# A tenth set of seven block products in a fused mixer layer, with decayed queries and keys kept in place

## The chip, the cores and the metric

One Trainium2 chip, one of its cores. The metric is the device time of one execution, in microseconds, from the first to the last instruction of the program and what lies around it. The kernel has the tensor engine (PE), the vector engine (DVE), the scalar engine (ACT), GpSimd (POOL) and the sync engine (SP) to itself; all data are float32 in HBM.

## The reference

One layer, 256 tokens, model width 2048. A normalised input is multiplied by one wide matrix, its columns are split into the operands of two mixers, and the mixers' results are projected, gated, summed and projected again:

```python
h = rmsnorm(x, pre_norm_g[l])
proj = h @ w_in[l]                      # 2048 x 18448
(a_q, a_k, a_v, a_g, a_lr, b_q, b_k, b_v, b_g, m_a, m_b) = jnp.split(proj, offsets, axis=-1)
gk = jax.nn.log_sigmoid((a_lr @ gla_gk_w2[l] + gla_gk_b[l])) / GATE_LOGIT_NORMALIZER
o_a = gla_chunked(...)                  # linear attention with a decay per key channel
o_a = rmsnorm(o_a, gla_norm_g[l]).reshape(B, S, GLA_VAL_DIM) * jax.nn.silu(a_g)
y_a = o_a @ w_branch_a[l]
o_b = diff_attention(...)               # difference of two softmax attentions
y_b = o_b @ w_branch_b[l]
merged = jax.nn.sigmoid(m_a) * y_a + jax.nn.sigmoid(m_b) * y_b
out = merged @ w_out[l]
x = x + rmsnorm(out, post_norm_g[l])
```

The 2048 columns of m_a, the gate of the linear-attention branch, are the ones that this change moves.

## The kernel before, in words

**Precision by splitting.** Each float32 weight block of 1024 columns per partition is split into a high and a low part: `hi` is a copy by ACT (line 356), `lo` is the rest, by a DVE subtraction (line 357). A product is three matmuls: hi by the input's high part, hi by its low part, lo by its high part. `hi` and `lo` have three buffers each, so a block can be split at most about two blocks ahead of its use. The unit of work is a *half step*: one split, and the matmuls that use it.

**Three kinds of half step.** In a token-major half tile (`half_tile`) 12 matmuls of 512 columns are made; in a channel-major one (`half_channel`) 8 of 512 and 8 of 256; both take as long. In a *set* a half step has 6 matmuls of 512, since a set multiplies blocks by seven products instead of eight (Winograd's form of Strassen's scheme): 1024 weight columns, seven products of 1024 x 512 blocks in the order `PRODUCTS = (1, 3, 5, 6, 2, 7, 4)`, each in four half steps (two tiles `t`, two halves `h`). Products 3, 5, 6 and 7 use sums of input blocks, kept as `s4`, `r1`, `s2`, `r3`. A set has 28 half steps, so 168 matmuls; the plain way takes 192 for the same 1024 columns.

**What a set costs beside matmuls.** Sums of weight blocks: some are made by an accumulating DMA on POOL's queue (line 249), eight per set by DVE, 1024 elements each (line 257, `a<-a,b` and `a<-a,c`). The DVE adds of products 7's tiles stand right behind each `lo` of product 7 in DVE's order. After product 6 and after product 7 DVE adds 512 columns of the product's bank to a kept one (`gr`, lines 880 and 889), both at a raised priority of the scheduler.

**The set phase.** `phase_steps` writes the order by hand: nine sets, and between their half steps 64 half steps of other work (*partners*): the last value columns, the linear attention's keys and queries, three of eight pairs of the other attention's heads. `PARTNERED` lists eight places in a set, each behind a (product, tile), that take a partner; `ALONE` takes places away. Before, set 0 has nine partners (two of them at its front), sets 1 to 7 have seven, set 8 has six. In this phase the order on PE is pinned.

**The phase after.** Plain work: two gates of 512 columns (`m02`, `m03`, 8 half tiles each), between them the five remaining head pairs (40 half tiles), then the projection `y0` (28 of its half tiles). Between these, *background tasks* get a turn: `pump(LANES)` gives the next step to each of the first three tasks of a list. A turn comes after every second half tile; a task that asked for it (`eager`) gets one in between. First in the list are `gla_scores(0)` and `(1)` (18 and 19 steps), then `gla_out`, then two lanes of the other attention. `gla_out` fetches values that were spilled (`vback`, on POOL's queue, in program order with the spills `dh` and `dl` of the heads), weighs them by the scores (line 526) and must be over when `y0` begins.

**Linear attention, before.** Scores come in seven levels of block size m = 1 to 64. Two running sums of log decays, `pre` and `suf`, are grown from level to level by DVE adds (lines 966, 967); at each level ACT takes their exponentials and DVE multiplies them into a copy of the queries (`xq`) and keys (`xk`). The products of `xq` and `xk` go to PE (line 982).

Of the kernel before, what the change touches and what calls it, by code (L numbers as in the profile page):

```python
# [10 lines left out]
AF = mybir.ActivationFunctionType  # L11
# [3 lines left out]
P = 128  # L15
# [11 lines left out]
ROWS = {"two": 2, "tok": 4, "chan": KT}  # L27
WARM = 10
PRODUCTS = (1, 3, 5, 6, 2, 7, 4)
SETS = 9  # L30
MERGE = (0, 1, 6)
GLA_GATES = (7, 8)
LEAD = 6
PAIRS = [(g, pair) for g in range(4) for pair in range(2)]
EARLY = 3
PARTNERED = ((1, 1), (3, 1), (5, 1), (6, 0), (6, 1), (2, 1), (7, 0), (7, 1))
SPILL_AT = (6, 0, 0)
ALONE = tuple((s, 6, 1) for s in range(9)) + ((8, 3, 1),)
# [15 lines left out]
def chunk_plan():  # L54

    plan = [("v0", "two", "w_in", [(6144, RANK), (2048, 2 * VG[0] - RANK)])]
    at = 2 * VG[0] - RANK
    for g, n in enumerate(VG[2:]):
        plan.append((f"v{g + 2}", "tok", "w_in", [(2048 + at, n)]))
        at += n  # L60
    for hf in range(2):
        for name, base in (("k", 1024), ("q", 0)):
            for c in range(4):
                plan.append((f"{name}{hf}{c}", "chan", "w_in", [(base + 512 * hf + P * c, P)]))
    o = 6144 + RANK
    for s in range(2):
        plan.append((f"set{s}", "set", "w_in", [(o + 10240 + 1024 * s, 1024)]))
    for s in range(2, 6):
        plan.append((f"set{s}", "set", "w_in", [(o + base + 512 * (s - 2), 512) for base in (4096, 6144)]))
    plan.append(("set6", "set", "w_in", [(o + 8192, 1024)]))  # L70
    for i, s in enumerate(GLA_GATES):
        plan.append((f"set{s}", "set", "w_in", [(4096 + 1024 * i, 1024)]))
    for g in range(4):
        for c in range(4):
            for n, name in enumerate(("dq", "dk")):
                plan.append((f"{name}{g}{c}", "chan", "w_in", [(o + 2048 * n + 512 * g + P * c, P)]))
        if g > 1:
            plan.append((f"m0{g}", "tok", "w_in", [(o + 8192 + 512 * g, 512)]))
        for br in range(2):
            kind = "late" if br and g < 2 else "tok"  # L80
            plan.append((f"y{br}{g}", kind, ("w_branch_a", "w_branch_b")[br], [(512 * g, 512)]))
        plan.append((f"o{g}", "late", "w_out", [(512 * g, 512)]))
    plan.append(("ys0", "half", "w_branch_b", [(c, 512) for c in BRANCH_COLS]))
    for s, cols in enumerate(LATE_COLS):
        plan.append((f"os{s}", "half", "w_out", [(c, 512) for c in cols]))
    return plan
# [56 lines left out]
def hybrid_kernel(ctx: ExitStack, tc, xt, xn, preg, postg, w, w2, gkb, glag, lamv, diffg, ident_d, causal_d, lmask_d, out):  # L143
# [57 lines left out]
    def halves_of(*keys):  # L201
        return [(key, r, h) for key in keys for r in range(len(at[key])) for h in range(2)]
# [2 lines left out]
        return halves_of(*(f"{name}{g}{c}" for g, pair in pairs for name in ("dq", "dk") for c in (2 * pair, 2 * pair + 1)))  # L205

    seq = halves_of("v0", "v2", "v3") + phase_steps()
    seq += halves_of("m02") + heads_order(PAIRS[EARLY:]) + halves_of("m03", *(f"y0{g}" for g in range(4)))[:-4]
    seq += branch_steps() + late_steps() + halves_of("o2", "o3")
    ready = {}  # L210
    emitted = [0]
# [288 lines left out]
        return xs[kt // 2][:, kt % 2].rearrange("p i t -> p (i t)")  # L500

    tasks = []
    ts, heads, m0 = {}, {}, []
    DONE = object()
    done = set()
    latest = [None]
# [49 lines left out]
    def half_tile(banks, n, q, ops, hi, lo, begin=0):  # L556
        for w, parts in ((hi, (0, 1)), (lo, (0,))):
            for j in range(2):
                kt = 2 * q + j
                a = ops(kt)  # L560
                for b in range(2):
                    for part in parts:
                        first, last = kt == begin and w is hi and part == 0, kt == KT - 1 and w is lo
                        i = mm(banks[b][:, :n], a[part][:, P * b : P * b + P], w[:, n * j : n * j + n], start=first, stop=last)
        latest[0] = i.ins

    def token_major(key, n, ops, step=1, upto=KT // 2):
        banks = [ps("mm"), ps("mm")]
        for q in range(upto):
            half_tile(banks, n, q, ops, *take(key))  # L570
            if q % 2 or not ts:
                pump(step)
            else:
                pump_eager()
        return banks

    def half_channel(o, h, hi, lo):
        turns = [(w, j) for w in (hi, lo) for j in range(8)]
        if h:
            turns.append(turns.pop(7))  # L580
        for w, j in turns:
            kt, c = 8 * h + j, slice(P * j, P * j + P)
            if w is hi:
                i = mm(o, hi[:, c], x_pair(kt), start=kt == 0, stop=kt == KT - 1)
            else:
                i = mm(o[:, :S], lo[:, c], x_ops(kt)[0], start=False, stop=False)
        latest[0] = i.ins

    def channel_major(key):
        o = ps("mm")  # L590
        for h in range(2):
            half_channel(o, h, *take(key))
            if h == 0:
                pump_eager()
        return o[:, :S], o[:, S:]

    def gate(bank, b, dst):
# [161 lines left out]
    def merge_gate(banks):
        t = u2([P, 2, 512], "mgate")  # L760
        for b in range(2):
            act.activation(t[:, b, :], banks[b], AF.Tanh, scale=half_rstd[:, b : b + 1])
        m0.append(spill(t, "mgate"))

    def head_part(t, o, o2, scaled):
        act.activation(t, o2, AF.Copy)
        dve.tensor_tensor(out=t, in0=o, in1=t, op=ALU.add)
# [155 lines left out]
    def gla_scores(hf):  # L923
# [1 line left out]
        if hf:  # L925
            yield
        pre = gp[hf]
        suf = u2([P, 2, 4, P], "suf")
        aall = u2([P, 3, 2, P], "att")
        a = aall[:, :2]  # L930
        ah, al = u2([P, 3, 2, P], "ath", F32R), u2([P, 3, 2, P], "atl", F32R)
# [12 lines left out]
        pool.memset(suf, 0.0)
        yield
        for n, m in enumerate(LEVELS):
            segs = 256 // m
# [4 lines left out]
            if m > 1:  # L952
                xk = t2([P, 512], "xk")
                xkv = view(xk, 0, (m, 2), (2 * m, segs), (1, m))
            act.activation(xqv, view(pre, m, *late), AF.Exp, scale=1.0 / 16.0)
            dve.tensor_tensor(out=xqv, in0=xqv, in1=view(q, m, *late), op=ALU.mult)
            if m == 1:
                dve.tensor_tensor(out=xqv, in0=xqv, in1=view(k, 0, *early), op=ALU.mult)
                add_pairs(es[:, 512:], xq, 64)
                act.activation(eh, es, AF.Copy)  # L960
                dve.tensor_tensor(out=el, in0=es, in1=f32(eh), op=ALU.subtract)
                pool.memset(a, 0.0)
            else:
                act.activation(xkv, view(suf, 0, *early), AF.Exp, scale=1.0 / 16.0)
                dve.tensor_tensor(out=xkv, in0=xkv, in1=view(k, 0, *early), op=ALU.mult)
            dve.tensor_tensor(out=view(suf, 0, *early), in0=view(suf, 0, *early), in1=view(pre, 2 * m - 1, (513 - 2 * m, 2), (2 * m, segs), (0, m)), op=ALU.add)
# [19 lines left out]
        xq = t2([P, 512], "xq")  # L986
        xk = t2([P, 512], "xk")
        flat = "p c t -> p (c t)"
        act.activation(xq, pre[:, 1].rearrange(flat), AF.Exp, scale=1.0 / 16.0)
        dve.tensor_tensor(out=xq, in0=xq, in1=q[:, 1].rearrange(flat), op=ALU.mult)  # L990
        act.activation(xk, suf[:, 0].rearrange(flat), AF.Exp, scale=1.0 / 16.0)
        dve.tensor_tensor(out=xk, in0=xk, in1=k[:, 0].rearrange(flat), op=ALU.mult)
        yield
# [665 lines left out]
```

## Time and profile before

| | |
|---|---|
| median of 3 runs | 1082.58 us (1082.48 to 1083.47) |
| the profiled execution's own time | 1083.89 us |
| its span | 1082.1 us |
| PE busy | 1073.0 us, 99% |
| DVE busy | 948.0 us, 88% |
| ACT busy | 741.8 us, 69% |
| DMA | 293.44 MB, mean 271 GB/s |

Busy time is the union of the instructions' spans, and matmuls overlap, so a busy PE may have short waits inside. A wait is better seen in the starts of the matmuls: where PE waits for nothing they follow at a fixed distance. The page numbers lines of the kernel before; the changed kernel's lines are some four to eleven higher.

### The profile page before, as it was taken

What the parts mean: (1) busy time and instruction counts of PE and PEld (TensorE: products, weight loads), DVE (VectorE), ACT (ScalarE), POOL (GpSimd) and SP (SyncE); (2) the same over time, 40 slices, a digit from 0 to 9 for tenths busy, and PEclk for the clock granted to TensorE, in tenths of its full rate; (3) what the DMA queues carried; (4) which work ended last, traced back from release to release, by engine and by line L of the source; (5) the groups of instructions that cost most, each with busy time, mean ns of one, the idle gap of its engine ahead of it and who ended that gap; (6) DMA issues with size and microseconds to landing.
All of it is one profiled execution on the core that took longest, in us unless ns stands there. A gap on an engine that the chain in (4) does not pass through costs nothing.

```text
span 1082.1 us, 15375 instructions
## 1 busy us (share of the span) xinstructions
PE 1073.0 (99%) x5404; PEld 919.1 (85%) x5404; DVE 948.0 (88%) x1282; ACT 741.8 (69%) x1068; POOL 168.1 (16%) x249
## 2 busy tenths in 40 slices
PE   9999999999999999999999999999999999999997
PEld 8998888888888888888888888888888888888886
DVE  7788999899999989998999999977778878889885
ACT  7987767677677767677777665556777776565662
POOL 0202121121212121212112200031011011100000
PEclk9999999999999999999999999999999999999999
DMA  9899889899989989898988766699898898988752
GB/s 346 285 324 300 261 250 345 206 311 271 276 291 212 332 202 390 177 381 188 350 190 274 295 226 205 211 325 302 285 278 276 279 288 277 319 302 259 276 191 91
DMA packets 67213, 293.44 MB, mean 271 GB/s; under 512 B 8704, under 2 KB 11776, under 8 KB 49984
## 3 DMA queue, kind: packets, MB, share of 16 engines
q1 hardware_dynamic: 38656, 174.29, 45.5%
q0 software_dynamic: 27904, 117.45, 40.1%
q8 instruction: 42, 0.69, 0.2%
q10 hardware_dynamic: 576, 0.73, 0.2%
q14 instruction: 35, 0.29, 0.1%
HBM read 265.17 MB, written 27.26 MB: 270 GB/s over the span
## 4 chain that ended last, share of the span: by engine, by line
PE 85%; issue 8%; DVE 3%; DMA 2%; POOL 1%; ACT 0%; POOLq 0%; SPq 0%; DVEq 0%; ACTq 0%
PE mm L553 57%; PE bg L553 20%; PE mm L541 2%; PE bg L541 2%; DVE lo L357 2%; DMA vback<-vl 1%; DMA raw<-in_w_dram 1%; PE bg L1149 0%; PE bg L1123 0%; PE bg L526 0%; PE bg L1124 0%; POOL dl L177 0%; DVE keep L357 0%; PE bg L1161 0%; PE bg L1162 0%
## 5 line engine op out<-in xcount | busy, mean ns | idle before, releaser
L356 ACT ACTIVATE hi<-raw 128x1024 fp32r<-128x1024 f32 (+3 forms) x229 | 234.8, 1028 | 152.9 <-PE mm L553 74.2
L357 DVE TENSOR_TENSOR lo<-raw,hi 128x1024 fp32r<-128x1024 f32 (+3 forms) x231 | 271.0, 1179 | 35.1 <-ACT hi L356 32.0
L356 ACT ACTIVATE hi<-a 128x1024 fp32r<-128x1024 f32 x144 | 152.5, 1061 | 54.8 <-PE mm L553 32.1
L357 DVE TENSOR_TENSOR lo<-a,hi 128x1024 fp32r<-128x1024 f32 x144 | 171.9, 1218 | 7.0 <-ACT hi L356 5.4
L553 PE MATMUL mm<-hi,xs 128*128 128x512 f32 (+1 forms) x688 | 174.7, 383 | 0.0
L553 PEld LDWEIGHTS mm<-hi,xs 128*128 128x128 f32 x688 | 128.5, 188 | 21.5
L553 PE MATMUL bg<-xs,hi 128*128 128x512 f32 x448 | 115.4, 390 | 0.0
L357 DVE TENSOR_TENSOR lo<-b,hi 128x1024 fp32r<-128x1024 f32 x72 | 87.9, 1221 | 18.0 <-ACT hi L356 16.0
L553 PE MATMUL mm<-lo,xs 128*128 128x512 f32 (+1 forms) x344 | 98.6, 383 | 0.1
L553 PEld LDWEIGHTS bg<-xs,hi 128*128 128x128 f32 x448 | 84.2, 188 | 16.4
L356 ACT ACTIVATE hi<-b 128x1024 fp32r<-128x1024 f32 x72 | 76.1, 1059 | 25.8 <-PE mm L553 13.7
L553 PE MATMUL mm<-xs,hi 128*128 128x512 f32 x320 | 84.9, 397 | 0.0
L553 PEld LDWEIGHTS mm<-lo,xs 128*128 128x128 f32 x344 | 64.2, 188 | 12.1 <-DVE lo L357 1.2
L553 PEld LDWEIGHTS mm<-xs,hi 128*128 128x128 f32 x320 | 57.7, 189 | 9.7
L553 PEld LDWEIGHTS bg<-xs,lo 128*128 128x128 f32 x448 | 61.0, 190 | 5.0 <-DVE lo L357 0.7
L553 PE MATMUL bg<-xs,lo 128*128 128x256 f32 x448 | 62.6, 283 | 0.3 <-DVE lo L357 0.3
L249 POOL DMA_DIRECT2D b<-in_w_dram x36 | 31.0, 861 | 152.7 <-DVE a L257 76.2
L356 ACT ACTIVATE hi<-c 128x1024 fp32r<-128x1024 f32 x36 | 38.2, 1062 | 21.5 <-PE bg L553 12.7
L553 PE MATMUL mm<-hi,oah 128*128 128x512 f32 x128 | 50.8, 397 | 0.0
L553 PE MATMUL mm<-hi,oal 128*128 128x512 f32 x128 | 50.0, 391 | 0.0
L357 DVE TENSOR_TENSOR lo<-c,hi 128x1024 fp32r<-128x1024 f32 x36 | 43.1, 1219 | 5.0 <-ACT hi L356 5.0
L553 PEld LDWEIGHTS mm<-xs,lo 128*128 128x128 f32 x320 | 43.6, 190 | 3.2
(410 smaller groups left out, 2218.5 us busy)
## 6 DMA issues: line engine op xcount, KB each, us to landing
raw<-in_w_dram SPq DMA_DIRECT2D x98, 1024.0 KB, 7.3
c<-in_w_dram SPq DMA_DIRECT2D x36, 512.0 KB, 8.9
a<-in_w_dram POOLq DMA_DIRECT2D x36, 512.0 KB, 9.7
b<-in_w_dram POOLq DMA_DIRECT2D x36, 512.0 KB, 7.3
a<-in_w_dram POOLq DMA_DIRECT2D x16, 1024.0 KB, 13.2
b<-in_w_dram POOLq DMA_DIRECT2D x16, 1024.0 KB, 8.7
raw<-in_w_dram SPq DMA_DIRECT2D x14, 832.0 KB, 7.4
gr<-gr POOLq DMA_DIRECT2D x9, 512.0 KB, 8.6
```

Source lines behind the costliest of these rows:

```text
L249: tc.keep_in_program_order(pool.dma_start(chain[s, name, i][:, c], block(s, 1, i)[:, c], accum_op=ALU.add))
L356: act.activation(hi_t[:, a:b], r[:, a:b], AF.Copy)
L357: dve.tensor_tensor(out=lo_t[:, a:b], in0=r[:, a:b], in1=f32(hi_t[:, a:b]), op=ALU.subtract)
L541: i = pe.matmul(banks[g][b][:, :n], a[part][:, P * b : P * b + P], w[:, n * g : n * g + n], start=first, stop=last)
L553: i = pe.matmul(*args, **kw)
```

## The change

Three things change.

1. The last 1024 columns of m_a (two plain gates of 512 columns) become a tenth set (set 7; the linear attention's gates move to sets 8 and 9). `merge_gate` goes, and the new set's two result tiles are spilled and fetched like those of set 6. The 64 partners stay, and now have ten sets: `ALONE` takes the place behind (2, 1) away from sets 2 to 9 and the place behind (6, 1) from all, so sets 2 to 9 have six partners each.
2. The linear attention keeps queries and keys decayed in place: at each level DVE multiplies `q` and `k` by a decay that ACT took from a sum of log decays over the level's segments (`total`, halved in width from level to level); `xq` and `xk` become copies by ACT.
3. Background turns come from `tick`: each half step adds 2/3 after its hi matmuls and 1/3 after its lo matmuls, and every 1.5 of this one turn is given to the first three tasks. The extra turns of eager tasks go.

```diff
-SETS = 9
-MERGE = (0, 1, 6)
-GLA_GATES = (7, 8)
+SETS = 10
+MERGE = (0, 1, 6, 7)
+GLA_GATES = (8, 9)
...
-ALONE = tuple((s, 6, 1) for s in range(9)) + ((8, 3, 1),)
+ALONE = tuple((s, 6, 1) for s in range(10)) + tuple((s, 2, 1) for s in range(2, 10))
+PACE = 1.5
...
-    seq += halves_of("m02") + heads_order(PAIRS[EARLY:]) + halves_of("m03", *(f"y0{g}" for g in range(4)))[:-4]
+    seq += heads_order(PAIRS[EARLY:]) + halves_of(*(f"y0{g}" for g in range(4)))[:-4]
...
+    beat = [0.0]
+
+    def tick(part):
+        if pinned[0] or not ts:
+            return
+        beat[0] += part
+        if beat[0] > PACE - 0.01:
+            beat[0] -= PACE
+            pump(LANES)
...
-            if q % 2 or not ts:
+            if not ts:
                 pump(step)
-            else:
-                pump_eager()
...
-            act.activation(xqv, view(pre, m, *late), AF.Exp, scale=1.0 / 16.0)
-            dve.tensor_tensor(out=xqv, in0=xqv, in1=view(q, m, *late), op=ALU.mult)
...
-            dve.tensor_tensor(out=view(suf, 0, *early), in0=view(suf, 0, *early), in1=view(pre, 2 * m - 1, (513 - 2 * m, 2), (2 * m, segs), (0, m)), op=ALU.add)
-            dve.tensor_tensor(out=view(pre, m, *late), in0=view(pre, m, *late), in1=view(pre, m - 1, (513, 2), (2 * m, segs), (0, m)), op=ALU.add)
+                act.activation(xqv, view(q, m, *late), AF.Copy)
+                act.activation(view(xk, 0, (m, 2), (2 * m, segs), (1, m)), view(k, 0, *early), AF.Copy)
+            if m < LEVELS[-1]:
+                dve.tensor_tensor(out=view(q, m, *late), in0=view(q, m, *late), in1=view(decay, 0, (512 // m + 1, 2), (2, segs), (0, m)), op=ALU.mult)
+                dve.tensor_tensor(out=view(k, 0, *early), in0=view(k, 0, *early), in1=view(decay, 1, (512 // m - 1, 2), (2, segs), (0, m)), op=ALU.mult)
+                pairs_of = total[:, : 1024 // m].rearrange("p (s i) -> p s i", i=2)
+                total = t2([P, 512], "total")
+                dve.tensor_tensor(out=total[:, : 512 // m], in0=pairs_of[:, :, 0], in1=pairs_of[:, :, 1], op=ALU.add)
+                act.activation(decay[:, : 512 // m], total[:, : 512 // m], AF.Exp, scale=1.0 / 16.0)
...
-    merge_gate(token_major("m02", 512, x_ops, LANES))
+    m0 = gspill[12:16]
     for g, pair in PAIRS[EARLY:]:
         diff_heads(g, pair)
-    merge_gate(token_major("m03", 512, x_ops, LANES))
```

How the instructions move is seen best on DVE, at two places of the same set (set 5). The first is between product 2 and product 7; `lo<-c` are the splits of product 2, `lo<-raw` a partner's, `lo<-b` product 7's, `a<-a,c` the sums of weight blocks. Before:

```order
L357 TENSOR_TENSOR lo_3725<-c_3608,hi_3724 128x1024
L357 TENSOR_TENSOR lo_3738<-c_3624,hi_3737 128x1024
L357 TENSOR_TENSOR lo_3748<-raw_3622,hi_3747 128x1024
L357 TENSOR_TENSOR lo_3760<-b_3312,hi_3759 128x1024
L257 TENSOR_TENSOR a_3196<-a_3196,c_3559 128x1024
L357 TENSOR_TENSOR lo_3773<-b_3312,hi_3772 128x1024
L257 TENSOR_TENSOR a_3196<-a_3196,c_3584 128x1024
```

The same place in the changed kernel:

```order
L357 TENSOR_TENSOR lo_3654<-c_3542,hi_3653 128x1024
L357 TENSOR_TENSOR lo_3667<-c_3556,hi_3666 128x1024
L357 TENSOR_TENSOR lo_3679<-b_3245,hi_3678 128x1024
L257 TENSOR_TENSOR a_3147<-a_3147,c_3489 128x1024
L357 TENSOR_TENSOR lo_3692<-b_3245,hi_3691 128x1024
L257 TENSOR_TENSOR a_3147<-a_3147,c_3518 128x1024
```

The partner between products 2 and 7 is gone, and its matmuls on PE with it. The second place is the end of product 7; `lo<-raw` is the split of the partner behind its second tile, `gr` the add at line 889 (894 in the changed kernel), which reads product 7's bank. Before:

```order
L357 TENSOR_TENSOR lo_3821<-b_3360,hi_3820 128x1024
L257 TENSOR_TENSOR a_3265<-a_3265,c_3624 128x1024
L357 TENSOR_TENSOR lo_3833<-raw_3770,hi_3832 128x1024
L889 TENSOR_TENSOR gr_3734<-mm_3449,p_237_3638 128x512
L357 TENSOR_TENSOR lo_3855<-a_3196,hi_3854 128x1024
```

The same place in the changed kernel:

```order
L357 TENSOR_TENSOR lo_3728<-b_3291,hi_3727 128x1024
L257 TENSOR_TENSOR a_3207<-a_3207,c_3556 128x1024
L894 TENSOR_TENSOR gr_3663<-mm_3381,p_233_3570 128x512
L357 TENSOR_TENSOR lo_3740<-raw_3689,hi_3739 128x1024
L357 TENSOR_TENSOR lo_3762<-a_3147,hi_3761 128x1024
```

The add now stands ahead of the partner's split. So it does in sets 2 to 9 of the changed kernel; in the kernel before it does so in set 0 alone (in set 0 of both).

More of the change, by code (lines that the diff above doesn't have):

```diff
@@ L69, in chunk_plan @@
         plan.append((f"set{s}", "set", "w_in", [(o + base + 512 * (s - 2), 512) for base in (4096, 6144)]))
-    plan.append(("set6", "set", "w_in", [(o + 8192, 1024)]))
+    for s in range(2):
+        plan.append((f"set{s + 6}", "set", "w_in", [(o + 8192 + 1024 * s, 1024)]))
     for i, s in enumerate(GLA_GATES):
@@ L76, in chunk_plan @@
                 plan.append((f"{name}{g}{c}", "chan", "w_in", [(o + 2048 * n + 512 * g + P * c, P)]))
-        if g > 1:
-            plan.append((f"m0{g}", "tok", "w_in", [(o + 8192 + 512 * g, 512)]))
         for br in range(2):
@@ L502, in hybrid_kernel @@
     tasks = []
-    ts, heads, m0 = {}, {}, []
+    ts, heads = {}, {}
     DONE = object()
@@ L564, in half_tile @@
                         i = mm(banks[b][:, :n], a[part][:, P * b : P * b + P], w[:, n * j : n * j + n], start=first, stop=last)
-        latest[0] = i.ins
+            latest[0] = i.ins
+            tick(2 / 3 if w is hi else 1 / 3)
     def token_major(key, n, ops, step=1, upto=KT // 2):
@@ L580, in half_channel @@
             turns.append(turns.pop(7))
-        for w, j in turns:
+        for n, (w, j) in enumerate(turns):
             kt, c = 8 * h + j, slice(P * j, P * j + P)
@@ L586, in half_channel @@
                 i = mm(o[:, :S], lo[:, c], x_ops(kt)[0], start=False, stop=False)
+            if n == 7:
+                latest[0] = i.ins
+                tick(2 / 3)
         latest[0] = i.ins
+        tick(1 / 3)
     def channel_major(key):
@@ L592, in channel_major @@
             half_channel(o, h, *take(key))
-            if h == 0:
-                pump_eager()
         return o[:, :S], o[:, S:]
@@ L757, in hybrid_kernel @@
     gspill = [None] * (2 * SETS)
[L759 to L763, printed above, removed]
     def head_part(t, o, o2, scaled):
@@ L927, in gla_scores @@
         pre = gp[hf]
-        suf = u2([P, 2, 4, P], "suf")
         aall = u2([P, 3, 2, P], "att")
@@ L940, in add_pairs @@
             dve.tensor_tensor(out=dst, in0=src[:, :, 0, :], in1=src[:, :, 1, :], op=ALU.add)
-        dve.tensor_tensor(out=suf, in0=q, in1=k, op=ALU.mult)
-        add_pairs(es[:, :512], suf.rearrange("p b c t -> p (b c t)"), P)
-        pool.memset(suf, 0.0)
+        flat4 = "p b c t -> p (b c t)"
+        own = u2([P, 2, 4, P], "own")
+        dve.tensor_tensor(out=own, in0=q, in1=k, op=ALU.mult)
+        add_pairs(es[:, :512], own.rearrange(flat4), P)
+        decay = u2([P, 1024], "decay")
+        act.activation(decay, pre.rearrange(flat4), AF.Exp, scale=1.0 / 16.0)
+        yield
+        dve.tensor_tensor(out=q, in0=q, in1=decay.rearrange("p (b c t) -> p b c t", b=2, c=4), op=ALU.mult)
+        total = pre.rearrange(flat4)
         yield
@@ L951, in gla_scores @@
             xqv = xq.rearrange("p (b s m) -> p b s m", b=2, m=m)
-            if m > 1:
-                xk = t2([P, 512], "xk")
-                xkv = view(xk, 0, (m, 2), (2 * m, segs), (1, m))
-            act.activation(xqv, view(pre, m, *late), AF.Exp, scale=1.0 / 16.0)
-            dve.tensor_tensor(out=xqv, in0=xqv, in1=view(q, m, *late), op=ALU.mult)
             if m == 1:
-                dve.tensor_tensor(out=xqv, in0=xqv, in1=view(k, 0, *early), op=ALU.mult)
+                dve.tensor_tensor(out=xqv, in0=view(q, m, *late), in1=view(k, 0, *early), op=ALU.mult)
                 add_pairs(es[:, 512:], xq, 64)
@@ L963, in gla_scores @@
             else:
-                act.activation(xkv, view(suf, 0, *early), AF.Exp, scale=1.0 / 16.0)
-                dve.tensor_tensor(out=xkv, in0=xkv, in1=view(k, 0, *early), op=ALU.mult)
-            dve.tensor_tensor(out=view(suf, 0, *early), in0=view(suf, 0, *early), in1=view(pre, 2 * m - 1, (513 - 2 * m, 2), (2 * m, segs), (0, m)), op=ALU.add)
-            dve.tensor_tensor(out=view(pre, m, *late), in0=view(pre, m, *late), in1=view(pre, m - 1, (513, 2), (2 * m, segs), (0, m)), op=ALU.add)
+                xk = t2([P, 512], "xk")
+                act.activation(xqv, view(q, m, *late), AF.Copy)
[7 more added lines that the diff above has]
+                act.activation(decay[:, : 512 // m], total[:, : 512 // m], AF.Exp, scale=1.0 / 16.0)
+            else:
+                last = ((2 * m, segs), (1, m))
+                dve.tensor_tensor(out=view(q, 512, *last), in0=view(q, 512, *last), in1=view(decay, 512 // m + 1, (2, segs), (0, m)), op=ALU.mult)
+                dve.tensor_tensor(out=view(k, 0, *last), in0=view(k, 0, *last), in1=view(decay, 1, (2, segs), (0, m)), op=ALU.mult)
             yield
@@ L985, in gla_scores @@
             yield
[L986 to L993, printed above, removed]
         bank = ps("bg")
@@ L996, in gla_scores @@
             for i in range(2):
-                c = slice(P * (2 * h + i), P * (2 * h + i) + P)
-                pe.matmul(bank[:, P * h : P * h + P], xk[:, c], xq[:, c], start=i == 0, stop=i == 1)
-        act.activation(aall[:, 2].rearrange(flat), bank[:, :S], AF.Copy)
+                c = 2 * h + i
+                pe.matmul(bank[:, P * h : P * h + P], k[:, 0, c], q[:, 1, c], start=i == 0, stop=i == 1)
+        act.activation(aall[:, 2].rearrange("p h t -> p (h t)"), bank[:, :S], AF.Copy)
         act.activation(ah, aall, AF.Copy)
@@ L1279, in diff_heads @@
                 head_part(t[:, c, :], *channel_major(f"{name}{g}{2 * pair + c}"), name == "dk")
-                pump(LANES)
             heads[g, pair, name] = split_spill(t)
@@ L1289, in b_ops @@
         return obh[kt // 4][:, kt % 4, :], obl[kt // 4][:, kt % 4, :]
-    m0.extend(gspill[12:14])
-    merge_gate(token_major("m02", 512, x_ops, LANES))
+    m0 = gspill[12:16]
     for g, pair in PAIRS[EARLY:]:
         diff_heads(g, pair)
-    merge_gate(token_major("m03", 512, x_ops, LANES))
     while "out" not in done:
```

## The prediction

> **What bounds the kernel now.** From the page the row of busy times, then one set of the set phase (set 5, 381.07 to 438.69) in the table by stage; its columns are the span, the busy time of PE, weight load, DVE, ACT and POOL, the granted clock, the DMA share and GB/s.
>
> ```profile
> PE 1073.0 (99%) x5404; PEld 919.1 (85%) x5404; DVE 948.0 (88%) x1282; ACT 741.8 (69%) x1068; POOL 168.1 (16%) x249
> 381.07:438.69 57.62, 57.62 (x281) 48.74 (x280) 53.34 (x51) 42.15 (x47) 11.86 (x17) 1.00 0.92 286
> ```
>
> PE is busy throughout, at full clock: the time is that of the matmuls. But DVE fills 53.34 of a set's 57.62 us, so PE runs free only while each `lo` is ready before PE asks for it. That lead is read by setting PE's timeline (start, duration) against DVE's in the same set, from the last half step of product 2 to the partner behind product 7:
>
> ```profile
> 408.51 1.07 PE L553 MATMUL mm<-hi,xs 128*128 128x512 f32 x4
> 409.87 1.07 PE L553 MATMUL mm<-hi,xs 128*128 128x512 f32 x4
> 410.77 0.62 PE L553 MATMUL mm<-lo,xs 128*128 128x512 f32 x2
> ...
> 414.93 0.62 PE L553 MATMUL mm<-lo,r3h 128*128 128x512 f32 x2
> 416.29 0.62 PE L553 MATMUL mm<-lo,r3h 128*128 128x512 f32 x2
> 418.56 1.11 PE L553 MATMUL bg<-xs,lo 128*128 128x256 f32 x8
> 420.44 0.62 PE L553 MATMUL mm<-lo,r3h 128*128 128x512 f32 x2
> 421.80 0.62 PE L553 MATMUL mm<-lo,r3h 128*128 128x512 f32 x2
> 423.84 1.12 PE L553 MATMUL bg<-xs,lo 128*128 128x256 f32 x8
> ```
>
> ```profile
> 407.01 2.35 DVE L357 TENSOR_TENSOR lo<-c,hi 128x1024 fp32r<-128x1024 f32 x2
> 409.55 1.22 DVE L357 TENSOR_TENSOR lo<-raw,hi 128x1024 fp32r<-128x1024 f32 x1 [0.19 <-ACT hi L356]
> 410.71 1.23 DVE L357 TENSOR_TENSOR lo<-b,hi 128x1024 fp32r<-128x1024 f32 x1
> 411.85 1.22 DVE L257 TENSOR_TENSOR a<-a,c 128x1024 f32<-128x1024 f32 x1
> 412.99 1.22 DVE L357 TENSOR_TENSOR lo<-b,hi 128x1024 fp32r<-128x1024 f32 x1
> 414.12 1.22 DVE L257 TENSOR_TENSOR a<-a,c 128x1024 f32<-128x1024 f32 x1
> 415.29 1.23 DVE L357 TENSOR_TENSOR lo<-raw,hi 128x1024 fp32r<-128x1024 f32 x1
> 416.44 0.42 DVE L767 TENSOR_TENSOR dq<-bg,dq 128x256 f32<-128x256 f32 x1
> 416.77 1.22 DVE L357 TENSOR_TENSOR lo<-b,hi 128x1024 fp32r<-128x1024 f32 x1
> 417.90 1.22 DVE L257 TENSOR_TENSOR a<-a,c 128x1024 f32<-128x1024 f32 x1
> 419.04 1.22 DVE L357 TENSOR_TENSOR lo<-b,hi 128x1024 fp32r<-128x1024 f32 x1
> 420.18 1.22 DVE L257 TENSOR_TENSOR a<-a,c 128x1024 f32<-128x1024 f32 x1
> 421.31 1.22 DVE L357 TENSOR_TENSOR lo<-raw,hi 128x1024 fp32r<-128x1024 f32 x1
> 422.45 0.69 DVE L889 TENSOR_TENSOR gr<-mm,p 128x512 f32<-128x512 f32 x1
> ```
>
> From start to start a half step takes PE 409.87 - 408.51 = 1.36 us (six matmuls of 0.227), a 1024-wide operation DVE 1.14, `gr` 0.6. The last `lo<-c` ends at 409.36 and is used at 410.77: a lead of 1.41. The partner's split costs DVE 1.16, but its matmuls hold PE for 2.77 (410.77 to 414.93, less a half step's 1.36, is 2.8), so the first `lo<-b`, ready at 411.94, has a lead of 2.99. Each half step of product 7 then makes DVE do a `lo` and an add, 2.27, against PE's 1.36: the lead falls by 0.91.
>
> **Part 1: the tenth set.** 192 matmuls become 168: 24 x 0.227 = **-5.4 us**, all on PE's path. The Trainium skill, in "TensorE: Matmul & The Clock Gate", section "Wait — 56ns, not 53.3ns?", gives a warm matmul N / 2.4 GHz + 2.5 ns, 215.7 ns here; by it the term would be -5.2, and the row decides. The set brings DVE 12 more splits, 8 sums and 3 `gr`-like adds, ACT 12 copies, POOL 12 loads; part 2 counts what that does. Loads, sums and the two spills come in the same rhythm as in other sets, DMA share 0.92; I take nothing for them.
>
> **Part 2: the partners respaced.** Sets 2 to 9 lose the partner between products 2 and 7, and `gr` moves ahead of the partner's split behind product 7. Walked with set 5's rows: the lead of 1.41 becomes 1.41 + 1.36 - 1.14 = 1.6 at the first `lo<-b` (not 2.99); 0.7 at the second; the partner's split keeps it (PE 416.29 to 418.56 = 2.27, DVE 2.27); the third gains 420.44 - 418.56 - 0.33 - 1.13 = +0.42, 1.1; the fourth 0.2. For the last partner PE gives 423.84 - 421.80 = 2.04, and DVE now owes sum, `gr` and split: 1.13 + 0.61 + 1.14 = 2.88. The lead is 0.84 short of need: PE waits 0.64. In general a set waits 2.24 us less the lead at the first `lo<-b`, which is 0.22 above that at the last `lo<-c`, but in an unbroken run of half steps not over some 1.6. While `gr` waits for product 7's last matmul, the partner's split and product 4's splits stand behind it on DVE, and PE waits for them.
>
> Other sets come with other leads. Before, the seven sets 2 to 8 have at the same place 0.87, 1.42, 0.88, 1.41, 0.06, 1.37 and 0.67; the rows of the first, the worst (set 6) and the last:
>
> ```profile
> 234.65 2.35 DVE L357 TENSOR_TENSOR lo<-c,hi 128x1024 fp32r<-128x1024 f32 x2
> 467.36 1.22 DVE L357 TENSOR_TENSOR lo<-c,hi 128x1024 fp32r<-128x1024 f32 x1
> 577.21 3.48 DVE L357 TENSOR_TENSOR lo<-c,hi 128x1024 fp32r<-128x1024 f32 x3
> ```
>
> ```profile
> 237.87 0.62 PE L553 MATMUL mm<-lo,xs 128*128 128x512 f32 x2
> 468.64 0.73 PE L553 MATMUL mm<-lo,xs 128*128 128x512 f32 x2
> 581.36 0.61 PE L553 MATMUL mm<-lo,xs 128*128 128x512 f32 x2
> ```
>
> That makes waits of 1.15, 0.64, 1.14, 0.64, 1.96, 0.65 and 1.35, on average 1.08. Eight sets: **+8.6 us**, between 8 x 0.64 = 5.1 and, since set 6 is one of seven, 8 x 1.5 = 12. Nothing hides it: with three buffers `lo` cannot be made earlier.
>
> That the order `gr`, then split, makes PE wait is seen in set 0, where it stands so already:
>
> ```profile
> 133.13 2.02 PE L553 MATMUL bg<-xs,hi 128*128 128x512 f32 x8
> 135.43 1.22 PE L553 MATMUL bg<-xs,lo 128*128 128x256 f32 x8 [0.29 <-DVE lo L357]
> ```
>
> ```profile
> 133.57 0.68 DVE L889 TENSOR_TENSOR gr<-mm,p 128x512 f32<-128x512 f32 x1
> 134.17 1.21 DVE L357 TENSOR_TENSOR lo<-raw,hi 128x1024 fp32r<-128x1024 f32 x1
> ```
>
> Eight matmuls from 133.13 end their turn at 134.95; the lo matmuls start at 135.43, 0.48 late, just behind DVE's split. The Trainium skill's same page, section "Architectural detail: the array is 16× 32×32, not 1× 128×128", says that DVE's queue is strictly first in, first out, so nothing slips past a `gr` that is not yet free; these rows agree. Could the split pass it, each set would wait 0.6 less, 4.9 in all, and the sum would end near no change.
>
> **Part 3: the linear attention.** DVE loses 58 operations of 512 and gets 28, two of 1024 and small sums; by
>
> ```profile
> L966 DVE TENSOR_TENSOR suf<-suf,gp 128x512 f32<-128x512 f32 x14 | 9.6, 685 | 0.6 <-POOL suf L944 0.6
> ```
>
> that is about 14 us less for DVE, two POOL fills less, and on PE as many score matmuls as before. It lies behind the heads' matmuls, where PE has one wait, below. I take 0; without cover (a task late for its turn) it would cost a step's chain, three such operations, some 2 us.
>
> **Part 4: turns every 1.5 half tiles.** The chain of 18 + 1 + 7 turns needs 26; 40 half tiles give 26, the last at 39, so it still ends before `y0`. But PE's one wait of that stage is for `vback`, fetched on POOL's queue behind the spill `dl`:
>
> ```profile
> 719.04 0.55 POOL L182 DMA_DIRECT2D vback<-vl  x1
> ```
>
> ```profile
> 731.45 0.50 PE L526 MATMUL bg<-vback,ath 128*128 128x512 f32 x1 [0.69 <-DMA vback<-vl]
> ```
>
> ```profile
> DMA to landing us min/median/max: 5.8/9.4/12.4
> ```
>
> This fetch took the 12.4. Between the head's last matmul, which frees `dl`, and this matmul PE's order has 50 matmuls of 512, 32 of 256 and 8 small ones before, 49, 25 and 4 after: about 1.9 us less cover (an estimate at 0.227, half of it and some 0.2 for a small one). **+1.9 us**; with a landing of 9.4 the wait of 0.69 goes, -0.7; with one that is late by as much again it is +3.8.
>
> **The sum.** -5.4 + 8.6 - 0.2 (an estimate of what set 6 waits already, whose lo matmuls start at 468.64 just as the split ends) + 1.9 = **+4.9** on the profiled execution's own 1083.89, which is 1.31 above the median of 1082.58: I say **1087.4** for the median.
>
> **The rivals.**
> - *The lead lasts.* By the table's row DVE needs 53.34 - 1.16 = 52.2 of 57.62 - 2.77 = 54.9 us in a set with six partners, so 5% are free, and set 8 had six. Then only PE's saving and the fetch count: -5.4 with 0 to +1.9, 1077.2 to 1079.1. Against it: set 8 kept the partner behind product 2, and in my walk DVE has no free moment in the stretch. It decides where the lead at the first `lo<-b` is over 2.2. Chance 0.15.
> - *Half of it.* Later half steps pay part back, each set waits about 0.6, the fetch waits as before: -5.4 + 4.8, 1082.0. Chance 0.13.
> - *The chain comes late.* If the linear attention's data lag its turns by two steps, PE stands before `y0`, or the fetch lands 5 us late; with two uncovered turns of 1.5 x 2.77 = 4.1 us on top of my sum, 1095. The granted clock is 1.00 in the row quoted. The Trainium skill's same page, section "HAM oscillation — how this bites in real kernels", says that a PE idle for over about 3.4 us falls to half clock; a wait that long would then cost about 1.7 us more, and no wait quoted here is long enough to show it. Chance 0.05.
> - My forecast: 0.67.
>
> The range: below, waits of 5.1 and no wait for the fetch give -1.0, 1081.6; above, waits of 12 and +3.8 give +10.2, 1092.8. It holds the second rival and leaves out the first and third, 0.2. A measurement of this kernel tells about 0.2%, 2.2 us, from no change. Faster: 0.15 and a little of the second rival, 0.17. Same: most of the second and the low end of mine, 0.18. Slower: 0.65.
>
> **What would show it.** In the profile after: 24 matmuls fewer; in each of sets 2 to 9 late lo matmuls behind product 7, with DVE's `lo` as the releaser, and a DVE without gaps there; sets of some 54.9 + 1.1 = 56 us; a wait of about 2.6 us at `vback`. I am wrong if lo matmuls in product 7 start on time, or if PE waits elsewhere.

## The result and the profile after

| | before | changed |
|---|---|---|
| median | 1082.84 us (1082.48 to 1083.47, 4 runs) | **1095.82 us** (1095.24 to 1097.31, 4 runs) |
| profiled execution, its span | 1083.89, 1082.1 us | 1097.31, 1095.3 us |

The ratio is 1.0121, 95% interval 1.0108 to 1.0133: slower by 13.0 us. The forecast was 1087.4, slower by 4.9, in a range of 1081.6 to 1092.8. The sign was right, the size was not.

The page of the changed kernel, the row of busy times and the shares of the chain that ended last:

```profile
PE 1076.5 (98%) x5380; PEld 913.2 (83%) x5380; DVE 960.1 (88%) x1289; ACT 755.6 (69%) x1090; POOL 174.8 (16%) x259
PE 84%; DVE 10%; issue 3%; ACT 1%; POOL 1%; DMA 0%; POOLq 0%; DVEq 0%; SPq 0%; ACTq 0%
```

PE issues 24 matmuls fewer (5404 to 5380), as it should, and is nevertheless busy 3.5 us longer, since the record of a matmul often covers part of a wait behind it (0.73 instead of 0.62 in a row below). DVE's share of the chain has grown to 10%. Where does PE wait? The view of waits, PE's rows (total, times, longest):

```profile
PE bg L563 <- DVE lo L357: 4.5, 9, 0.6
PE mm L1185 <- DVE ogb L1179: 3.1, 3, 1.3
...
PE bg L1156 <- DVE prob L1151: 1.3, 2, 1.0
...
PE mm L563 <- DVE lo L357: 1.2, 3, 0.6
```

The first and the last row are the forecast's waits for `lo` in the sets. The two between them are of the other attention's lanes, which the forecast didn't have at all. And `vback`, before a row of 0.7 and in the forecast one of about 2.6, is gone.

This view counts only what a record shows as idle. The whole loss is seen in the matmul starts: from each distance to the next start take the median distance of its width, and add up what is left. Where zero lies depends a little on how the widths are grouped (in `y0` by about 1 us), so the differences count. By stretch, in us:

| stretch | before | changed | difference |
|---|---|---|---|
| first matmuls (up to 20 us) | 1.05 | 2.66 | +1.6 |
| set phase | 2.93 | 14.05 | **+11.1** |
| heads, up to the weighing of `vback` | 0.79 | 1.54 | +0.75 |
| weighing of `vback` | 1.05 | 0.10 | -0.95 |
| `y0` (760 to 900 us) | -0.50 | 6.12 | **+6.6** |
| the last stretch | 2.68 | 1.87 | -0.8 |
| 24 matmuls at 0.227 | | | -5.4 |
| sum | | | +12.9 |

The spans differ by 13.2; this execution stands 1.5 above its kernel's median, that of before 1.0, and the first matmuls differ from one execution to the next (run 2 below loses 0.7 there, not 2.66). Two stretches carry the rest.

**The sets.** The changed kernel's set 5, from the start of its product 7 to the start of the next set's, and the end of product 7 between: first PE, then DVE.

```profile
409.20 0.39 PE L563 MATMUL mm<-hi,r3h 128*128 128x512 f32 x1
...
417.01 0.73 PE L563 MATMUL mm<-lo,r3h 128*128 128x512 f32 x2
417.58 1.77 PE L563 MATMUL bg<-xs,hi 128*128 128x512 f32 x7
419.88 0.39 PE L563 MATMUL bg<-xs,lo 128*128 128x256 f32 x1 [0.53 <-DVE lo L357]
...
465.15 0.39 PE L563 MATMUL mm<-hi,r3h 128*128 128x512 f32 x1
```

```profile
415.74 1.22 DVE L357 TENSOR_TENSOR lo<-b,hi 128x1024 fp32r<-128x1024 f32 x1
416.88 1.22 DVE L257 TENSOR_TENSOR a<-a,c 128x1024 f32<-128x1024 f32 x1
418.01 0.68 DVE L894 TENSOR_TENSOR gr<-mm,p 128x512 f32<-128x512 f32 x1
418.61 1.21 DVE L357 TENSOR_TENSOR lo<-raw,hi 128x1024 fp32r<-128x1024 f32 x1
```

The rows are as forecast: DVE without a gap, sum, `gr`, split, and PE's lo matmuls just behind the split, at 419.88, 0.69 later than they would follow. The set takes 465.15 - 409.20 = 55.95 us. (The other distances from product 7 to product 7, for sets 2, 3, 4, 6, 7 and 8, are 56.97, 56.13, 56.13, 56.39, 56.15 and 56.50.)

**The stretch of `y0`.** One of its waits, on PE, DVE and ACT. The scores whose probabilities are turned at 809.00 end with the first row.

```profile
797.22 0.28 PE L1131 MATMUL bg<-kl,q 128*128 128x256 f32 x1
...
801.00 0.49 PE L1156 MATMUL bg<-ident,prob 128*128 128x128 f32 x3
...
807.60 0.39 PE L1169 MATMUL bg<-dv,prob 128*128 128x128 f32 x2
809.00 0.83 PE L1156 MATMUL bg<-ident,prob 128*128 128x128 f32 x3 [1.01 <-DVE prob L1151]
```

```profile
802.31 0.61 DVE L1179 SCALAR_TENSOR_TENSOR ogb<-bg,de,ub 128x128 f32<-128x128 f32 x2 [0.80 <-POOL de L459]
802.83 0.28 DVE L1136 CUSTOM_DVE_ANT_0 prob<-bg,causal 128x128 f32<-128x128 f32 x1
...
805.68 0.15 DVE L1137 TENSOR_TENSOR mx<-mx,neg_scale 128x4 f32<-128x4 f32 x1
...
807.43 0.58 ACT L1142 ACTIVATE prob<-prob,mx,score_scale 128x256 f32<-128x256 f32 x1
...
808.59 0.75 DVE L1151 SCALAR_TENSOR_TENSOR prob<-prob,c,prob 128x128 f32<-128x128 f32 x2
```

The reader follows one lane: the scores end at 797.50; DVE takes their maxima only from 802.83, behind another lane's `ogb`, which waited for POOL; the maxima are scaled at 805.68, ACT's last exponential ends at 808.01, DVE's `prob` lets PE go at 809.00. That is 11.5 us from scores to transposes. The transposes stand two turns behind the scores in PE's order, and two turns of 1.5 half tiles are 2 x 1.5 x 2.77 = 8.3 us, with the lanes' own matmuls some 10. PE waits.

The row with the larger total, `ogb`, is of a chain of one turn only: from the weighting of a head's values, over ACT, DVE, POOL and DVE again, to the transposes of the result.

```profile
831.44 0.39 PE L1169 MATMUL bg<-dv,prob 128*128 128x128 f32 x2
...
837.10 0.59 PE L1185 MATMUL mm<-ident,ogb 128*128 128x128 f32 x2 [0.87 <-DVE ogb L1179]
```

The weighting ends at 831.83, so the chain takes 5.3 us, and the half tiles of one turn last 1.5 x 2.77 = 4.2.

### The profile page after: what moved, and what is told of

The parts are those of the page before. It is cut to its first block, busy times and chain, and to the rows that moved or that the text cites. A ratio compares the mean times of both kernels' runs of the same rounds, so it can differ in the third digit from the quotient of the medians.

```text
span 1095.3 us, 15378 instructions
## 1 busy us (share of the span) xinstructions
PE 1076.5 (98%) x5380; PEld 913.2 (83%) x5380; DVE 960.1 (88%) x1289; ACT 755.6 (69%) x1090; POOL 174.8 (16%) x259
## 4 chain that ended last, share of the span: by engine, by line
PE 84%; DVE 10%; issue 3%; ACT 1%; POOL 1%; DMA 0%; POOLq 0%; DVEq 0%; SPq 0%; ACTq 0%
PE mm L563 57%; PE bg L563 18%; DVE lo L357 5%; DVE a L257 3%; PE mm L551 2%; PE bg L551 2%; PE bg L997 1%; PE mm L536 1%; PE bg L536 1%; ACT prob L1142 1%; POOL de L459 1%; DVE gr L894 1%; DMA raw<-in_w_dram 0%; ACT hi L356 0%; DVE prob L1136 0%
## 5 line engine op out<-in xcount | busy, mean ns | idle before, releaser
L356 ACT ACTIVATE hi<-raw 128x1024 fp32r<-128x1024 f32 (+3 forms) x213 | 218.0, 1027 | 117.7 <-PE mm L563 69.9
L357 DVE TENSOR_TENSOR lo<-raw,hi 128x1024 fp32r<-128x1024 f32 (+3 forms) x215 | 252.5, 1179 | 39.9 <-ACT hi L356 35.9
L356 ACT ACTIVATE hi<-a 128x1024 fp32r<-128x1024 f32 x160 | 169.6, 1060 | 79.6 <-PE bg L563 35.7
L357 DVE TENSOR_TENSOR lo<-a,hi 128x1024 fp32r<-128x1024 f32 x160 | 191.6, 1220 | 7.6 <-ACT hi L356 6.1
L563 PE MATMUL mm<-hi,xs 128*128 128x512 f32 (+1 forms) x608 | 155.7, 382 | 0.0
L563 PEld LDWEIGHTS mm<-hi,xs 128*128 128x128 f32 x608 | 113.9, 188 | 18.7
L357 DVE TENSOR_TENSOR lo<-b,hi 128x1024 fp32r<-128x1024 f32 x80 | 97.8, 1222 | 20.2 <-ACT hi L356 17.8
L356 ACT ACTIVATE hi<-b 128x1024 fp32r<-128x1024 f32 x80 | 84.4, 1058 | 24.5 <-PE mm L563 14.4
L563 PE MATMUL mm<-lo,xs 128*128 128x512 f32 (+1 forms) x304 | 88.9, 382 | 0.1
L257 DVE TENSOR_TENSOR a<-a,b 128x1024 f32<-128x1024 f32 x40 | 48.9, 1221 | 0.6
```

The costliest lines, as they stand in the source:

```text
L257: add = dve.tensor_tensor(out=a, in0=a, in1=chain[s, "b", i][:, c] if second else raws[s, i, h], op=ALU.add)
L356: act.activation(hi_t[:, a:b], r[:, a:b], AF.Copy)
L357: dve.tensor_tensor(out=lo_t[:, a:b], in0=r[:, a:b], in1=f32(hi_t[:, a:b]), op=ALU.subtract)
L563: i = pe.matmul(*args, **kw)
```

## The experiments

Two theories came out of this, and a rival to each. *Place*: the sets wait because the partner behind product 2 is gone just where DVE's lead is made; rival: DVE has too much to do in a set with six partners, wherever they are. *Spacing*: lanes get their turns too soon; rival: DVE's queue makes them late at any spacing. A ratio here is always to the kernel before, run beside it on the same chip (medians 1082.36 to 1082.61).

**1. Turns every 2 half tiles once the linear attention is over.**

```
-        if beat[0] > PACE - 0.01:
-            beat[0] -= PACE
+        pace = 2 if "out" in done else PACE
+        if beat[0] > pace - 0.01:
+            beat[0] -= pace
```

> The changed kernel, but once the linear attention is over a turn comes every 2 half tiles, as before the change. Theory (turns too close): in the stretch of y0 (760 to 900 us) the changed kernel's lane matmuls wait for probabilities that are not ready 1.5 half tiles (4.2 us) after the scores; matmul starts there are 6.6 us later in sum than before the change. With 5.5 us between turns these waits go: 1089 to 1091, a little of it given back if the lanes end later. Rival (the lanes are late because DVE has more queued in this stretch, whatever the spacing): the same waits, 1095 to 1097. The set phase keeps its 11 us of waits in both.

1105.63 us, 1.0214 (1.0198 to 1.0229): 10 us slower than the changed kernel. Neither number came. But the stretch in question did what the theory said: by matmul starts 760 to 880 us lose -0.35 where the changed kernel loses 4.7. The time is lost behind it:

```profile
PE mm L1186 <- DVE ogb L1180: 3.8, 1, 3.8
PE bg L1131 <- DVE ogb L1180: 3.0, 1, 3.0
PE mm L564 <- ACT hi L356: 2.4, 1, 2.4
...
PE bg L1126 <- ACT prob L1159: 1.5, 1, 1.5
```

All four lie between 900 and 940 us: the lanes have not ended when the branches need them, and PE stands through their last steps with nothing beside them, 16 us in all by matmul starts. So the spacing does set the waits in `y0`, and the number of turns has a floor. These long waits also show a second price, PE's rows behind the wait of 3.0 and the table by stage (span; busy PE, weight load, DVE, ACT, POOL; granted clock, DMA share, GB/s):

```profile
913.49 0.58 PE L1131 MATMUL bg<-kh,q 128*128 128x256 f32 x1 [2.97 <-DVE ogb L1180]
...
914.51 0.63 PE L564 MATMUL mm<-hi,oah 128*128 128x512 f32 x1
914.94 0.63 PE L564 MATMUL mm<-hi,oal 128*128 128x512 f32 x1
```

```profile
914.00:918.50 4.50, 4.50 (x14) 3.63 (x13) 1.48 (x11) 2.57 (x9) 0.50 (x1) 0.50 0.95 162
```

A matmul of 512 now takes 0.427 (914.94 - 914.51), not 0.227, at a granted clock of 0.50: ten of them, 2.0 us on top of the wait.

**2. The partner left out behind product 1 instead of product 2.**

```
-ALONE = tuple((s, 6, 1) for s in range(10)) + tuple((s, 2, 1) for s in range(2, 10))
+ALONE = tuple((s, 6, 1) for s in range(10)) + tuple((s, 1, 1) for s in range(2, 10))
```

> The changed kernel, but sets 2 to 9 leave out the partner behind product 1 in place of the one behind product 2. The number of partners, sets and half steps is the same. Theory (the partner between products 2 and 7 is what gives DVE its lead): the waits at the partner behind product 7 and in product 7 go, 10 to 11 us less, 1084 to 1086. Rival (DVE has too much to do in a set with six partners, wherever they stand): the waits move to another place, 1094 to 1097.

1084.59 us, 1.0020 (1.0011 to 1.0029). The theory's number: 11 us less from one digit. By matmul starts the set phase loses some 3.7 us instead of 14. Set 5 now takes 458.52 - 403.68 = 54.84 us:

```profile
403.68 0.40 PE L563 MATMUL mm<-hi,r3h 128*128 128x512 f32 x1
...
458.52 0.40 PE L563 MATMUL mm<-hi,r3h 128*128 128x512 f32 x1
```

DVE is as busy as in the changed kernel (960.2 to 960.1 us). The rival falls: it isn't how much DVE does, but where PE gives it time. The edit also moves `gr` back behind the partner's split in DVE's order, by itself, so it doesn't part the two causes that the forecast had for a set's wait; run 5, beside this one, does.

**3. The same with product 3** (`(s, 3, 1)` in that line).

> As the run before, but the place left out in sets 2 to 9 is the one behind product 3. Theory: the waits behind product 7 go here too; the lead at product 5 is the next to be short, about 1 us in all: 1085 to 1087. Rival (only the sum of DVE's work counts): 1094 to 1097. If the two runs differ by more than 2 us, each place has a price of its own.

1087.28 us, 1.0043 (1.0028 to 1.0058), just above the theory's number. Of the waits behind product 7 one is left, 0.6 in set 8, where `gr` stands ahead of the split again. Three new ones of 0.2 to 0.4 stand at a partner's lo matmuls elsewhere, and inside product 5 of set 5 PE waits 0.6 for ACT's `hi` (0.5 in run 2). A place has its own price, 2.7 us between these two.

**4. and 5. `gr` behind product 7 later in DVE's order.**

```
                         if prod == 7:
-                            with tc.high_priority(offset=100):
+                            with tc.high_priority(offset=1):
```

> The changed kernel with one thing changed: the addition gr behind product 7 has no raised priority, so that in DVE's order it stands two or three splits further back, behind the split of the partner. Theory of the prediction (the gr ahead of the split costs 0.61 in each of eight sets): 5 us less, 1090 to 1092; the waits of 0.2 to 0.8 at product 7's own lo stay. Rival 1 (DVE owes the same work before product 4 in either order): 1094 to 1097. Rival 2 (product 4's first matmul, which overwrites the bank that gr reads, now waits for gr): 1096 or more.

1108.44 us, 1.0237 (1.0220 to 1.0254): rival 2, some 12 us above the least it named. The view of waits, and the longest of them in PE's rows:

```profile
PE mm L563 <- DVE gr L894: 15.6, 10, 2.8
```

```profile
138.22 2.05 PE L563 MATMUL mm<-hi,xs 128*128 128x512 f32 x4 [2.80 <-DVE gr L894]
```

Product 4 overwrites the bank that `gr` reads, and `gr` stood behind three splits. This went too far to test the forecast's claim, so the next run moves `gr` back by one place only, with an offset of 25. It sets this offset also at the same add of the sets in the last stretch (line 1459); the loss there stays the same within 0.1 us.

> The changed kernel, with gr behind product 7 moved back by one place in DVE's order in every set, from ahead of the partner's split to just behind it (in the run before it stood behind three splits, and product 4 waited for it). Theory of the prediction: the split can start 0.61 earlier, so each wait of 0.69 at the partner's matmuls shrinks to about 0.1; gr ends under 2 us after product 7 while product 4 starts 2.8 after it and doesn't wait: 8 x 0.61 = 4.9 less, 1090 to 1092. Rival (what DVE owes before product 4 is the same in either order, and the wait comes out there): 1094 to 1097.

1090.03 us, 1.0066 (1.0050 to 1.0081): 5.8 us less than the changed kernel, 4.8 of it in the set phase by matmul starts. Set by set it is the forecast's 0.61: the set that took 56.13 takes 55.53, set 5 takes 460.74 - 405.41 = 55.33 instead of 55.95. PE's rows and DVE's in set 5:

```profile
413.78 1.78 PE L563 MATMUL bg<-xs,hi 128*128 128x512 f32 x7
415.49 1.21 PE L563 MATMUL bg<-xs,lo 128*128 128x256 f32 x8
```

```profile
414.22 1.22 DVE L357 TENSOR_TENSOR lo<-raw,hi 128x1024 fp32r<-128x1024 f32 x1
415.35 0.68 DVE L894 TENSOR_TENSOR gr<-mm,p 128x512 f32<-128x512 f32 x1
```

The partner's lo matmuls follow its hi matmuls without a wait, and `gr` ends before product 4 needs its bank. So of the 1.1 to 1.3 us that an ordinary set waits in the changed kernel, 0.6 is the order of `gr` and the split, and the other 0.5 to 0.7, still there in this run, is the partner's place: in run 2 the order in sets 2 to 9 is the same as here, only the place differs, and set 5 takes 54.84 instead of 55.33.

**6. and 7. Run 2 with two spacings**, 1.5 and then 1.75, and 1.25 and then 2 (the numbers in the lines of run 1).

> The partner behind product 1 left out, as in the second run, and turns every 1.5 half tiles only until the linear attention is over, every 1.75 (4.8 us) after that. Theory (turns too close for a lane's chain from scores to probabilities): the waits of 6 us in the stretch of y0 shrink to 0 to 3, and the lanes still end before the branches, unlike with 2: 1079 to 1082. Rival 1 (the lanes are late by then, as with 2): 1088 or more. Rival 2 (the waits don't hang on the spacing): 1084 to 1086.

1081.85 us, 0.9984 (0.9974 to 0.9994).

> As the run before, but turns every 1.25 half tiles (3.5 us) until the linear attention is over and every 2 after that, so about as many in all. Theory: the waits in the stretch of y0 are gone, as in the first run, and the lanes, which start earlier, end in time; the linear attention's steps, some 2 us of DVE and ACT, keep up or cost up to 2 us in all: 1079 to 1081. Rival (its steps, or the fetch of the values, are late at 3.5 us): 1083 or more, with waits between 650 and 760 us.

1081.87 us, 0.9989 (0.9980 to 0.9999). Run 6 lies in its theory's range, run 7 0.9 us above its own. Both are 2.7 us less than run 2 and ahead of the kernel before by one or two tenths of a per cent. They are the lowest here, but run 9 below (0.9993) can't be told from them. In `y0` (760 to 920 us, by matmul starts) run 2 loses 6.2, spacing 1.75 loses 3.4 and spacing 2 loses 1.1: the waits follow the spacing. Run 7 pays some of it back between 640 and 680 us, where its linear attention has turns every 3.5 us and loses 2.3 us instead of 0.7.

**8. The changed kernel with the old linear attention**, and **9. the kernel before with the new one alone.** Run 8 takes the body of `gla_scores` from before, run 9 puts the new one into the kernel before.

> The changed kernel with the linear attention as it was before the change, all else the same. Theory of the prediction (it lies behind the heads' matmuls, 14 us of DVE are worth nothing): 1095 to 1097. Rival (at turns every 4.2 us the old steps, with three 512-wide DVE operations more and two exponentials in each, are late for their turns): waits of 3 to 8 us between 680 and 760 us, 1099 to 1104; then the rewrite is what makes the closer turns possible.

1104.82 us, 1.0203 (1.0186 to 1.0220), the rival, 0.8 us above its range: 9 us slower than the changed kernel.

```profile
750.77 0.47 PE L536 MATMUL bg<-vback,ath 128*128 128x512 f32 x1 [1.73 <-DMA vback<-vh]
753.86 0.80 PE L536 MATMUL bg<-vback,ath 128*128 128x512 f32 x1 [2.62 <-DMA vback<-vl]
...
759.69 0.79 PE L536 MATMUL bg<-vback,ath 128*128 128x512 f32 x1 [0.76 <-DMA vback<-vl]
```

The releaser is the fetch of the values, not the steps themselves, and from 754 to 763 us the granted clock is 0.50. That the old steps make this fetch late is shown; by which of their waits was not taken apart.

> The kernel before with the new linear attention alone: nine sets, partners and turns as before. Theory (at a turn every 5.5 us with extra turns in between, the old steps already kept up, so 14 us less of DVE are worth nothing): within 1 us of before, 1081.5 to 1083.5. Rival (DVE is what holds the heads' stage): 3 to 8 us faster, 1075 to 1079.

1081.92 us, 0.9993 (0.9984 to 1.0002): nothing, with DVE 13.5 us less busy than before:

```profile
PE 1072.3 (99%) x5404; PEld 918.7 (85%) x5404; DVE 934.5 (86%) x1266; ACT 744.7 (69%) x1076; POOL 166.6 (15%) x247
```

So the rewrite is worth nothing at the old spacing, as forecast, and 9 us at the new one.

**10., 11., 12. Other spacings for run 2**: 1.4 and 1.9; 1.375 and 2; eight turns of 1.5, then 1.25, then 2.

> The partner behind product 1 left out, turns every 1.4 half tiles until the linear attention is over and every 1.9 (5.3 us) after it. Theory (a turn's distance of over 5 us covers a lane's chain, one of 3.9 us covers a linear attention step): waits of under 1 us between 640 and 700 and under 1.5 between 760 and 900, the lanes end in time: 1079.5 to 1081. Rival (waits of some 2 us come back in whichever stretch is squeezed): 1081.5 to 1084.

1084.84 us, 1.0021 (1.0012 to 1.0030).

> As the run before with 1.375 and 2. Theory: the waits between 760 and 900 go below 1, as with 1.25 and 2, and those between 640 and 700 shrink from 2.3 to about 1; with 16 turns after the linear attention the lanes still end in time: 1079 to 1080.5. Rival (two turns are missing at the end, PE stands at the branches, clock and all): 1085 to 1095.

1083.99 us, 1.0008 (0.9999 to 1.0017).

> The partner behind product 1 left out; the first eight turns every 1.5 half tiles, then every 1.25 until the linear attention is over, then every 2. Theory: the waits of 2 us between 655 and 680 that 1.25 brought were in the first turns and go; those of the stretch of y0 stay under 1; if the fetch of the values meets its turn as with 1.25, the time is 1079 to 1081. Rival 1 (the fetch's wait of 2 to 2.5 us comes back, as with 1.375 and 1.4, since it hangs on where its turn falls): 1081.5 to 1084. Rival 2 (no gain beyond the runs with 1.5 and 1.75 or 1.25 and 2): 1081.5 to 1082.5.

1085.10 us, 1.0023 (1.0014 to 1.0031). None met its theory: runs 10 and 12 end about 1 us above the fetch's or the squeezed stretch's rival, run 11 between its two. The losses in `y0` (760 to 900 us) are 3.0, 0.1 and 1.1, but PE waits for the fetch of the values instead, 1.9 in run 10, 2.3 in run 11 and 3.8 in run 12. Run 12's row, and its clock behind it:

```profile
730.69 0.70 PE L538 MATMUL bg<-vback,ath 128*128 128x512 f32 x2 [3.77 <-DMA vback<-vh]
```

```profile
731.50:735.00 3.50, 3.50 (x11) 2.84 (x10) 0.00 (x0) 1.75 (x3) 0.00 (x0) 0.53 1.13 418
```

Runs 6 and 7 don't have this wait. None of the spacings that were run avoids it and the lanes' waits at once better than runs 6 and 7 do.

## Why the prediction was right in sign and wrong in size

- **Part 1, the tenth set, -5.4: right.** 5380 matmuls stand against 5404, at the same 0.227. In run 2, where the sets hardly wait, five of the seven distances from product 7 to product 7 are 54.84 us (the others 55.04 and 55.81), the forecast's 54.9.
- **Part 2, the partners, +8.6: right mechanism, +11.1 measured.** Place, releaser, DVE's gapless rows and the 0.61 of the order of `gr` (run 5) are as told; run 5 and run 2 show both causes apart. What was mis-sized is the lead that the walk starts from. It was taken over from the kernel before, where set 5 has 1.41 at its last `lo<-c`. Set 5 of the changed kernel, DVE and PE:

```profile
405.52 2.35 DVE L357 TENSOR_TENSOR lo<-c,hi 128x1024 fp32r<-128x1024 f32 x2
407.79 1.22 DVE L357 TENSOR_TENSOR lo<-b,hi 128x1024 fp32r<-128x1024 f32 x1
```

```profile
408.75 0.62 PE L563 MATMUL mm<-lo,xs 128*128 128x512 f32 x2
...
410.11 0.62 PE L563 MATMUL mm<-lo,r3h 128*128 128x512 f32 x2
```

  Its lead there is 0.88 (407.87 to 408.75), and 1.10 at the first `lo<-b` (409.01 to 410.11), not 1.6. The forecast's rule, 2.24 less this lead, then gives 1.14, and the set does take 55.95 - 54.84 = 1.11 more than in run 2. Over sets 2 to 8 the lead at the last `lo<-c` is 0.59 on average, where the forecast had 0.95; the rule with the leads as they are gives waits of 1.55, and 1.48 came. So the rule held and its input was off by 0.36 in each of eight sets, 2.9 us. (With less lead PE also waits at the second split of product 7, up to 0.78 in set 2.) Why a set comes with less lead was not taken apart; in run 2, with as many partners, sets 2 to 9 come with about 1.4. The forecast's sets of "some 54.9 + 1.1 = 56 us" are 56.3 on average. Against 8.6 less the 0.2 of set 6 this is 2.7 of the 8.1 us that the forecast missed; it lay inside the bounds of 5.1 to 12.
- **Part 3, the linear attention, 0: right.** DVE lost 13.5 us (forecast 14) and the time didn't move (run 9). The reason given, that it lies behind the heads' matmuls, holds only for the old turns: run 8 shows that the new turns need it.
- **Part 4, the turns, +1.9: this step failed.** It asked whether 26 turns fit before `y0` and priced the one wait that the heads' stage had, at `vback`. It took nothing, and gave no reason, for what the closer turns do inside `y0`, where the two lanes live: +6.6, most of the miss. The trace of before could have told it. There the 16 chains from a head's scores to its first probabilities take 5.1 to 11.4 us, 6.4 in the median, and the transposes follow the scores after 11.7 to 14.3 us; in the changed kernel they follow after 9.4 to 12.5, waits included. (The chains grew too, to 8.0 in the median; at the spacing of run 1 it is 6.6.) At `vback` the wait went instead of growing. The third fetch, which was waited for before, and its first use:

```profile
749.87 0.55 POOL L182 DMA_DIRECT2D vback<-vl  x1
...
759.25 0.63 PE L536 MATMUL bg<-vback,ath 128*128 128x512 f32 x2
```

  From 749.87 to 759.25 it has 9.4 us, where before it had 11.7 (719.04 to 731.45, less the wait): 2.3 less cover, near the forecast's 1.9. But it landed after 5.5 us, not after 12.4. So the count was right and the landing was the open term; the lower end that the forecast named for it, -0.7, came out (-0.95). That such a wait can come is shown by runs 8 and 10 to 12, which have it.
- **The rivals.** "The lead lasts" and "half of it" are refuted by the sets' 56.3 us. "The chain comes late" named 1095, and 1095.8 came, but by luck and not by its path: neither the linear attention nor the fetch is late, and the clock isn't lost either (the longest of the quoted waits is 1.3, the granted clock of the execution 0.999). The forecast's own test, "I am wrong if ... PE waits elsewhere", is what happened.
- **The sum with the measured terms**: -5.4 + 11.1 + 6.6 - 0.95 + 0.75 = 12.1; the rest to 12.9 is the first matmuls (+1.6), which belong to this one execution, and the last stretch (-0.8).

Not tried: more than three buffers for `lo`, which would test the lead directly; and the turns every 1.5 half tiles in a kernel with nine sets.

## What to carry to other kernels

When partners hide an engine's backlog, their place matters more than their number: moving one partner in each of eight sets was worth 11 us, at the same DVE load. When background steps get their turns more often, each chain that spans turns has to be measured against the new spacing in every stage that has such turns, not only in the one for whose sake they were made closer; too far apart costs as well, once the steps run out of cover. A step whose saving is hidden today may be what makes a tighter order possible tomorrow, so its worth is tested in the new order too.

## What the runs showed of the hardware

- **A wait of under 3 us is enough to halve PE's clock.** After waits of 2.80 (run 4) and 2.97 us (run 1) a 512-wide matmul takes up to 0.427 us for 3 to 5 us, a further 1.5 to 2 us; the granted clock is 0.59 over 138 to 142 us of run 4. In run 8 it is 0.50 behind a wait of 2.62, which one of 1.73 preceded. After 2.31 (run 11) and 2.4 us (run 1, at 903 us) the clock stays at 1.00. The Trainium skill, "TensorE: Matmul & The Clock Gate", section "HAM oscillation — how this bites in real kernels", puts the limit at idle gaps of about 3.4 us; in these runs shorter ones were enough, and they agree with the halved clock. These cases are too few to give a limit.
- **The halving can come after the wait.** In run 12 the first matmuls behind a wait of 3.77 run at full speed, and the clock is low from 731.5 to 735 us, when PE is busy again.
